# The feed-forward of a decoder layer by 2x2 blocks: seven products in place of eight

## The chip, the core and the metric

The kernel runs on one core of one Trainium2 chip. The metric is the device time of one launch in microseconds. Before the change it is 1752.19 us, the median of three runs (1750.87 to 1752.77).

## What is computed

One pre-norm decoder layer on 1024 tokens of width 1024, in float32: four causal token mixers with gates and an output projection, then a SwiGLU feed-forward of hidden width 2816, then a final RMSNorm. The change concerns the second sub-layer and its neighbours.

```python
D_MODEL = 1024; SEQ = 1024; FFN_HIDDEN = 2816; RMS_EPS = 1e-6

def rmsnorm(x, g):
    y = x * lax.rsqrt(jnp.mean(x * x, axis=-1, keepdims=True) + RMS_EPS)
    return y * g

def hybrid_layer(x, ...):
    h = rmsnorm(x, norm1_g)
    ...
    x = x + merged @ w_o
    h2 = rmsnorm(x, norm2_g)
    g_ff, up_ff = jnp.split(h2 @ w_gate_up, 2, axis=-1)
    return x + (jax.nn.silu(g_ff) * up_ff) @ w_down

def reference(x, ...):
    return rmsnorm(hybrid_layer(x, ...), final_g)
```

## The kernel before

Matrix products are made of float32r operands. `split` (L126) cuts a float32 tile into a high part (a cast on ScalarE) and a low part (a subtraction on VectorE), and `mm3` (L119) adds high by high, high by low and low by high in one PSUM bank, so a float32 product of 128 x 128 by 128 x 512 costs three matmuls (L122 to L124). Weights are laid out on the host in blocks of 128 rows by 1024 float32, loaded on SyncE's queue and split by `load_w` (L111).

The program runs through norm1, the mixers, and then twice, once for each half of 512 tokens, through the gates, the merge and the output projection `wo` (`tok_out`, L645). `evict_o` (L730) adds its PSUM banks to x; the sum, x2, lies in a tile of pool `gp` and is stored to DRAM as `x2d` on SyncE's queue. For the first half of tokens, norm2 (`norm_T`, L164) runs beside the second half's gates. The second half's x2 is loaded back from `x2d` in the feed-forward and its norm2 runs there (L745), each of its four tiles of 128 tokens with eight transposes on TensorE in two PSUM banks.

The feed-forward (L750 to L810) runs once for each half of tokens. A hidden block of 128 channels needs two weight blocks, gate and up, of 8 x 3 matmuls each (`group`, L174); Silu on ScalarE, a product on VectorE and a split give `fft`, which stays in SBUF. Then `tok_out` multiplies by `wd`, 11 weight blocks for each 512 output columns, four PSUM banks at once. The feed-forward has 2112 matmuls in gate and up and 1056 in down, 3168 in all, and 32 transposes. The last evictions, the final norm and the stores of `out` are the tail (L782 to L808).

Engines run their instructions in the order in which the program writes them, after a list scheduler has merged what the loops issue; within one engine nothing passes an instruction that waits. Tiles of a pool tag rotate through a fixed number of buffers, and a pool that is closed gives its memory to the next one, whose tiles wait for whatever last used that memory.

## Time and profile before

| | |
|---|---|
| median of three runs | 1752.19 us |
| profiled execution | 1752.49 us |
| its span, first to last instruction | 1750.5 us |
| mean granted TensorE clock | 0.998 |
| feed-forward, first matmul to last | 1006.57 to 1743.5 us |
| PE busy, share of the span | 1714.4 us, 98% |

The profiled execution has its own time, 1752.49 us: 1750.5 us of span and 2.0 us around it. It lies 0.3 us above the median. PE is TensorE's matmuls, PEld its weight loads (which overlap them), DVE VectorE, ACT ScalarE, POOL GpSimd and SP SyncE. A matmul's record in the timeline is longer than the distance to the next one, since matmuls are pipelined; the rate is read from counts in windows.

### The profile page before, as it was taken

The page shows a single profiled execution, that of the slowest core. Times are in us where ns is not written, and L with a number is a line of the kernel's source. Part 1 is how long each engine was busy: PE and PEld are TensorE (multiplying, and loading weights), DVE is VectorE, ACT ScalarE, POOL GpSimd, SP SyncE. Part 2 cuts the span into 40 slices and gives each one's busy share as a digit, 9 for nine tenths or more (in the row PEclk, how much of TensorE's full clock was granted, in tenths as well). Part 3 has the DMA queues.
Part 4 walks back from the last instruction along what each step waited for, and adds up shares of the span by engine and source line. Part 5 has one row for each costly group of instructions (what it writes and reads, how often), then busy time and mean ns, then how long its engine had stood idle before and what let it go on. Part 6 is the DMA issues. An engine that isn't in the chain of part 4 may idle for free.

```text
span 1750.5 us, 19973 instructions
## 1 busy us (share of the span) xinstructions
PE 1714.4 (98%) x7973; PEld 1392.1 (80%) x7973; DVE 816.4 (47%) x1168; ACT 605.9 (35%) x975; POOL 57.3 (3%) x124
## 2 busy tenths in 40 slices
PE   7999999999999999999999999999999999999998
PEld 7778777777788888888888888888888888888886
DVE  6676778777624345343436353333323333333232
ACT  5433456655432222243222142222212322222222
POOL 2011011010000000000000000000000000000000
PEclk9999999999999999999999999999999999999999
DMA  4311110111242224442223363222222522222222
GB/s 179 106 55 49 66 32 22 31 32 33 79 132 97 95 87 143 145 132 97 96 97 134 105 242 109 96 89 93 96 96 97 192 97 96 94 90 94 97 96 97
DMA packets 52620, 171.22 MB, mean 98 GB/s; under 512 B 6160, under 2 KB 9264, under 8 KB 52528
## 3 DMA queue, kind: packets, MB, share of 16 engines
q1 hardware_dynamic: 51952, 167.85, 28.6%
q10 hardware_dynamic: 576, 2.10, 0.4%
q8 instruction: 63, 1.03, 0.2%
q14 instruction: 29, 0.24, 0.0%
HBM read 156.27 MB, written 13.65 MB: 97 GB/s over the span
## 4 chain that ended last, share of the span: by engine, by line
PE 87%; DVE 4%; issue 1%; ACT 1%; POOL 0%; POOLq 0%; DVEq 0%; ACTq 0%
PE mmf L124 9%; PE mmf L123 9%; PE mmf L122 9%; PE mmg L124 7%; PE mmg L123 7%; PE mmg L122 7%; PE acc L124 6%; PE acc L122 6%; PE acc L123 6%; PE mm L124 3%; PE mm L122 3%; PE mm L123 3%; PE o L399 2%; PE pr L123 2%; PE pr L122 2%; PE pr L124 2%
## 5 line engine op out<-in xcount | busy, mean ns | idle before, releaser
L128 DVE TENSOR_TENSOR wlo<-wraw,whi 128x1024 fp32r<-128x1024 f32 x250 | 306.1, 1224 | 601.9 <-ACT whi L127 595.3
L127 ACT CAST whi<-wraw 128x1024 fp32r<-128x1024 f32 x250 | 262.1, 1048 | 863.2 <-PE mmf L123 320.0
L124 PE MATMUL mmf<-g0h,wlo 128*128 128x512 f32 x352 | 139.2, 396 | 0.0
L124 PE MATMUL mmf<-g1h,wlo 128*128 128x512 f32 x352 | 139.2, 395 | 0.0
L123 PE MATMUL mmf<-g1l,whi 128*128 128x512 f32 x352 | 138.7, 394 | 0.0
L123 PE MATMUL mmf<-g0l,whi 128*128 128x512 f32 x352 | 138.7, 394 | 0.0
L122 PE MATMUL mmf<-g0h,whi 128*128 128x512 f32 x352 | 138.5, 393 | 0.0
L124 PE MATMUL acc<-whi,fft 128*128 128x512 f32 x352 | 138.4, 393 | 0.0
L122 PE MATMUL acc<-whi,fft 128*128 128x512 f32 x352 | 138.3, 393 | 0.0
L122 PE MATMUL mmf<-g1h,whi 128*128 128x512 f32 x352 | 138.2, 393 | 0.0
L123 PE MATMUL acc<-wlo,fft 128*128 128x512 f32 x352 | 137.4, 390 | 0.0
L124 PE MATMUL mmg<-h1h,wlo 128*128 128x512 f32 x256 | 101.4, 396 | 0.1
L124 PE MATMUL mmg<-h0h,wlo 128*128 128x512 f32 x256 | 101.3, 396 | 0.0
L123 PE MATMUL mmg<-h0l,whi 128*128 128x512 f32 x256 | 100.9, 394 | 0.0
L123 PE MATMUL mmg<-h1l,whi 128*128 128x512 f32 x256 | 100.8, 394 | 0.0
L122 PE MATMUL mmg<-h1h,whi 128*128 128x512 f32 x256 | 100.8, 394 | 0.0
L122 PE MATMUL mmg<-h0h,whi 128*128 128x512 f32 x256 | 100.4, 392 | 0.0
L761 DVE TENSOR_TENSOR sl<-mmf,sl 128x512 f32<-128x512 f32 x44 | 30.4, 691 | 150.1 <-PE mmf L124 150.1
L122 PEld LDWEIGHTS mmf<-g1h,whi 128*128 128x128 f32 x352 | 66.6, 189 | 15.3
L122 PEld LDWEIGHTS mmf<-g0h,whi 128*128 128x128 f32 x352 | 66.6, 189 | 15.1
L123 PEld LDWEIGHTS mmf<-g1l,whi 128*128 128x128 f32 x352 | 66.1, 188 | 15.5
L123 PEld LDWEIGHTS mmf<-g0l,whi 128*128 128x128 f32 x352 | 66.1, 188 | 15.3
(253 smaller groups left out, 3187.8 us busy)
## 6 DMA issues: line engine op xcount, KB each, us to landing
wraw<-in_wgu_dram SPq DMA_DIRECT2D x88, 512.0 KB, 3.2
wraw<-in_wgate_dram SPq DMA_DIRECT2D x64, 512.0 KB, 3.2
wraw<-in_wd_dram SPq DMA_DIRECT2D x44, 512.0 KB, 3.2
wraw<-in_wmix_dram SPq DMA_DIRECT2D x22, 512.0 KB, 3.3
wraw<-in_wbr_dram SPq DMA_DIRECT2D x16, 512.0 KB, 3.2
wraw<-in_wo_dram SPq DMA_DIRECT2D x16, 512.0 KB, 3.2
xt<-in_x_dram SPq DMA_DIRECT2D x8, 512.0 KB, 9.2
yr<-ydr SPq DMA_DIRECT2D x8, 512.0 KB, 4.3
```

Of the source, the lines that this page charges most:

```text
L122: nc.tensor.matmul(o, ah, bh, start=start, stop=False)
L123: nc.tensor.matmul(o, ah, bl, start=False, stop=False)
L124: nc.tensor.matmul(o, al, bh, start=False, stop=stop)
L127: nc.scalar.copy(hi, v)
L128: nc.vector.tensor_sub(lo, v, hi.bitcast(F32))
L399: nc.tensor.matmul(o, vv[:, s0 + s, j, :], pt[:, i, s * 256:(s + 1) * 256], start=s0 + s + i == 0, stop=s0 + s + i == ns)
L761: nc.vector.tensor_mul(sl, ou, sl)
```

## The change

The feed-forward's three large products are each taken as 2x2 blocks and computed with seven block products and sums of blocks (Winograd's form), instead of eight. For gate and up, the activations are the four blocks of (token half, upper or lower 512 of the width), and each step g of 22 takes 256 of the weights' columns: seven products of 12 matmuls. For down, the blocks are (token half, even or odd hidden block) against (even or odd hidden block, 512 output columns): seven products of 11 x 12 matmuls. In all 154 x 12 + 7 x 132 = 2772 matmuls, 396 fewer.

```diff
-                nc.sync.dma_start(x2d[4 * half + t], x2[t])
+                (nc.gpsimd if half else nc.sync).dma_start(x2d[4 * half + t], x2[t])
...
+    EARLY = 10
+    def tile4(name):
+        return fp.tile([P, 1024], F32, tag="x4", name=name, bufs=10)
+    def tile2(name):
+        return fp.tile([P, HT], F32, tag="x2", name=name, bufs=6)
+    def four(s, x11, x12, x21, x22, first):
+        if first:
+            tt(s[0], x21, x22, op=add)
+            tt(s[1], s[0], x11, op=sub)
+            tt(s[2], x11, x21, op=sub)
+            tt(s[3], x12, s[1], op=sub)
...
     def norm2(t):
...
+        nc.gpsimd.dma_start(xa, xnd[t - 4])
+        nc.gpsimd.dma_start(r, x2d[t])
...
+        four(s, a0, b0, a1, b1, False)
+        yield
+        for v, to in zip([b1] + s, (h22, t1, t2, t3, t4)):
+            tr = pq.tile([P, 512], F32, tag="tr", name="trn", bufs=2).rearrange("p (k t) -> p k t", k=4)
+            for k in range(4):
+                nc.tensor.transpose(tr[:, k, :], v[:, k * P:(k + 1) * P], identf)
+            split(to[0][:, :, c], to[1][:, :, c], tr)
+    def pair_w(n=1024):
+        return [fp.tile([P, n], F32R, tag=f"w{v}{n}", name=f"w{v}", bufs=4 if n == 1024 else 1) for v in "hl"]
+    def prod(w, h):
+        o = pq.tile([P, HT], F32, tag="pp", name="pp", bufs=6)
...
+    def early(g, w):
+        nc.scalar.copy(p1, prod(half_of(w, 0), h11))
+        tt(sl, prod(half_of(w, 1), h21), p1, op=add)
+        nc.scalar.activation(sl, sl, AF.Silu)
+        nc.gpsimd.dma_start(stash[g][:, :512], p1)
+        nc.gpsimd.dma_start(stash[g][:, 512:], sl)
...
+    def rest(g, w):
...
+        tt(u2, prod(w[6], t2), p1, op=add)
+        tt(u3, prod(w[7], t3), u2, op=add)
+        p5 = prod(w[5], t1)
+        tt(u2, p5, u2, op=add)
+        tt(up, p5, u3, op=add)
+        tt(u3, prod(w[4], t4), u3, op=add)
+        tt(u2, prod(w[3], h22), u2, op=add)
+        nc.scalar.activation(u2, u2, AF.Silu)
+        nc.vector.tensor_mul(ff[:, 0], u3, sl)
+        nc.vector.tensor_mul(ff[:, 1], up, u2)
+    def down_a(j, e, o):
+        four(halves(s[0]) + halves(s[1]), e[:, 0], o[:, 0], e[:, 1], o[:, 1], True)
+        q.dma_start(ffd[j][:, 0], e[:, 0])
...
+    def down_b(j):
...
+        four(halves(s[0]) + halves(s[1]), r[0][:, :512], r[1][:, :512], r[0][:, 512:], r[1][:, 512:], False)
+            nc.gpsimd.dma_start(wdd[j][:, 3 + 2 * i:5 + 2 * i], s[i].rearrange("p (t c) -> p t c", t=2))
...
+    ready = [prepared(0), prepared(2)]
...
+        for g in range(EARLY):
+            early(g, ready.pop(0))
+            if g + 2 < EARLY:
+                ready.append(prepared(2 * g + 4))
+            if g % 2 == 0 and 1 <= g // 2 < 4:
+                next(turns[g // 2])
+            if g % 2 == 0 and g:
+                next(turns[g // 2 - 1], None)
+    nxt = blocks_w(0)
+    for g in range(NF):
+        w = nxt
+        if g + 1 < NF:
+            nxt = blocks_w(g + 1)
+        ff = rest(g, w)
+        if g % 2 == 0:
+            down_b(g // 2)
+            last = ff
+        else:
+            down_a(g // 2, last, ff)
...
+    def fetch(na, nb, j):
+        v = []
+        for src in (ffd[j][:, na], wd_of(nb, j)):
+            v.append(dn.tile([P, HT], F32, tag="dr", name="dr", bufs=8))
+            nc.sync.dma_start(v[-1], src)
+        return v
+    def operand(r):
+        hl = dn.tile([P, 2, HT], F32R, tag="dhl", name="dhl", bufs=10)
+        split(hl[:, 0], hl[:, 1], r)
+        return hl[:, 0], hl[:, 1]
+    def product(na, nb, stagger=0, raw=None):
+        acc = [pd.tile([P, HT], F32, tag="acc", name="acc", bufs=8) for _ in range(4)]
...
```

The stages of the new feed-forward are these. **Early**: products 1 and 2, which need only the first half of tokens, for the steps 0 to 9, 20 products in all; their results go to DRAM (`stash`) on GpSimd's queue. After the steps 2, 4, 6 and 8 of these stands one turn of norm2: four tiles of 128 tokens, each with five groups of four transposes in two PSUM banks (`tr`), 80 transposes in all. **Rest, steps 0 to 9**: five products each. **Rest, steps 10 to 21**: seven products each. In every step VectorE also makes four block sums of the weights (`four` in `blocks_w`) and, by turns, four of the down weights (`down_b`) or of the activations (`down_a`); these go to DRAM (`wdd`, `ffd`) on GpSimd's queue, in four or in seven pieces of 256 KB. **Down**: seven products of 11 steps j; each j loads two tiles of 256 KB from DRAM on SyncE's queue and splits both; eight PSUM banks hold two products; block results are added by VectorE, some by GpSimd.

Memory: the pools of the weights and of the feed-forward's tiles are closed and opened so that new tiles lie over old ones. In the built program the first weights' high part (`wh_8019`) begins at byte 137,216 of each partition, and the tile that holds x2's last two token tiles (`x2_7708`) ends at byte 137,600. The cast that writes `wh_8019` therefore waits for two stores on GpSimd's queue, those of `x2d` 6 and 7.

**ScalarE where the feed-forward begins.** The names `whi` and `wh` are high parts of weights, `raw` their float32, `pp` and `mmf` PSUM banks of products. Before:

```order
L127 CAST whi_7898<-wraw_7896 128x1024
L127 CAST whi_7928<-wraw_7926 128x1024
L127 CAST whi_7970<-wraw_7968 128x1024
L127 CAST whi_8001<-wraw_7999 128x1024
L127 CAST whi_8062<-wraw_8060 128x1024
```
After the change:

```order
L134 CAST whi_7906<-wraw_7904 128x1024
L134 CAST whi_7936<-wraw_7934 128x1024
L913 DMA wh_8031<-in_norm2_g_dram 128x512
L913 DMA wl_8032<-in_norm2_g_dram 128x512
L134 CAST wh_8019<-raw_8021 128x1024
L134 CAST wh_8025<-raw_8027 128x1024
L159 ACTIVATE xn2_8039,ss_8040<-x2r_8037 128x1024
L839 COPY p1_8052<-pp_8054 128x512
```
The last cast of `wo` (`whi_7928` before, `whi_7936` now) was followed by casts of gate and up weights into buffers of their own. Now the loads of norm2's weights and the cast of `wh_8019`, the one that waits for the two stores, follow it, and all that ScalarE does for the feed-forward stands behind.

**VectorE in the first norm2 turn.** `trn` are the transposes' PSUM banks, `g1l` and `t2l` to `t4l` the low parts that they end in, `tok` the sums of token blocks. Before:

```order
L128 TENSOR_TENSOR wlo_8094<-wraw_8091,whi_8093 128x1024
L147 TENSOR_SCALAR ss_8130<-ss_8130 128x1
L128 TENSOR_TENSOR g1l_7703<-trn_8046,g1h_7702 128x4x128
L128 TENSOR_TENSOR g1l_7703<-trn_8053,g1h_7702 128x4x128
L166 SCALAR_TENSOR_TENSOR xn2_8129<-x2r_8127,ss_8130,g_sb_8036 128x1024
```
After the change, from the scaling of the second token tile (whose part `wl_8164` of a weight stands just ahead) to the end of the first turn:

```order
L793 SCALAR_TENSOR_TENSOR xn2_8173<-x2r_8171,ss_8174,wl_8032 128x512
L778 TENSOR_TENSOR tok_8180<-xn2_8173,xa2_8169 128x512
L840 TENSOR_TENSOR sl_8131<-pp_8146,p1_8130 128x512
L779 TENSOR_TENSOR tok_8180<-xn2_8173,tok_8180 128x512
L780 TENSOR_TENSOR tok_8181<-xn2_8173 128x512
L781 TENSOR_TENSOR tok_8181<-xa2_8169,tok_8180 128x512
L135 TENSOR_TENSOR g1l_7711<-trn_8186,g1h_7710 128x4x128
L135 TENSOR_TENSOR g1l_7711<-trn_8193,g1h_7710 128x4x128
L135 TENSOR_TENSOR t2l_7982<-trn_8200,t2h_7981 128x4x128
L135 TENSOR_TENSOR t3l_7984<-trn_8207,t3h_7983 128x4x128
L135 TENSOR_TENSOR wl_8255<-raw_8256,wh_8254 128x1024
L135 TENSOR_TENSOR t4l_7986<-trn_8214,t4h_7985 128x4x128
```
Two low parts for a tile of 128 tokens became five (`g1l` for the block itself and for its first sum, `t2l` to `t4l` for the other sums). Ahead of the first of them stand the scalings and sums of the next tile of tokens (`tok_8180`, `tok_8181`) and the eviction of a product 2 (`sl_8131`), and a weight's low part (`wl_8255`) stands among them.

**VectorE where gate and up give way to down.** `ff` is the activation of a step, `fs` the sums for down, `dhl` the split operands of down's first steps j. Before, in the first half of tokens, the split activation `fft` was the operand itself, and the weights of down (from `wlo_9594` on) were split ahead:

```order
L761 TENSOR_TENSOR sl_9538<-mmf_9513,sl_9538 128x512
L128 TENSOR_TENSOR wlo_9594<-wraw_9591,whi_9593 128x1024
L128 TENSOR_TENSOR fft_9473<-sl_9538,fft_9473 128x512
L128 TENSOR_TENSOR wlo_9624<-wraw_9621,whi_9623 128x1024
L128 TENSOR_TENSOR wlo_9654<-wraw_9651,whi_9653 128x1024
```
After the change:

```order
L882 TENSOR_TENSOR u2_11469<-pp_11529,u2_11469 128x512
L886 TENSOR_TENSOR ff_11544<-up_11513,u2_11469 128x512
L773 TENSOR_TENSOR fs_11547<-ff_11423,ff_11544 128x512
L775 TENSOR_TENSOR fs_11548<-ff_11423 128x512
L774 TENSOR_TENSOR fs_11547<-fs_11547,ff_11423 128x512
L776 TENSOR_TENSOR fs_11548<-ff_11544,fs_11547 128x512
L135 TENSOR_TENSOR dhl_11591<-dr_11575,dhl_11591 128x512
L135 TENSOR_TENSOR dhl_11594<-dr_11577,dhl_11594 128x512
L135 TENSOR_TENSOR dhl_11613<-dr_11609,dhl_11613 128x512
```
The low parts of the first j, which down's first product needs (`dhl_11591` and `dhl_11594`), stand behind the last step's two evictions (`u2_11469` and `ff_11544`, which waits for Silu) and the four sums of `down_a`.

## Rows read from the trace of the kernel before

**Rows 1.** The profile's page: busy time, share and instructions; then the last chain.
```profile
PE 1714.4 (98%) x7973; PEld 1392.1 (80%) x7973; DVE 816.4 (47%) x1168; ACT 605.9 (35%) x975; POOL 57.3 (3%) x124
...
PE 87%; DVE 4%; issue 1%; ACT 1%; POOL 0%; POOLq 0%; DVEq 0%; ACTq 0%
```

**Rows 2.** The waits view: engine and tile, awaited, us in total, times, longest us.
```profile
ACT whi L127 <- PE mmf L123: 320.0, 82, 4.3
...
PE o L399 <- DVE pt L128: 13.0, 11, 1.9
```

**Rows 3.** Windows: start and end us, length, busy time (count) per engine, PEclk, DMA share, GB/s.
```profile
1006.57:1254.90 248.33, 247.88 (x1088) 201.63 (x1087) 91.65 (x103) 79.31 (x104) 2.19 (x4) 1.00 0.36 123
...
1621.40:1743.50 122.10, 122.07 (x530) 99.07 (x528) 35.86 (x43) 28.81 (x38) 1.31 (x3) 1.00 0.27 90
...
1400.00:1600.00 200.00, 200.00 (x865) 162.51 (x864) 67.23 (x73) 57.32 (x73) 0.00 (x0) 1.00 0.29 95
```

**Rows 4.** Timeline of PE in norm2: start us, length, line, operation, count, idle before.
```profile
1020.85 1.07 PE L161 MATMUL trn<-identf,xn 128*128 128x128 f32 x8 [0.45 <-DVE xn L166]
```

**Rows 5.** Timeline around the feed-forward's start, by engine: PE, DVE, ACT.
```profile
1006.34 0.39 PE L124 MATMUL acc<-whi,mgt 128*128 128x512 f32 x1
1006.57 0.39 PE L122 MATMUL mmf<-g0h,whi 128*128 128x512 f32 x1
...
1005.39 0.69 DVE L732 TENSOR_TENSOR x<-acc,x 128x512 f32<-128x512 f32 x1 [0.67 <-PE acc L124]
...
1006.77 0.69 DVE L732 TENSOR_TENSOR x<-acc,x 128x512 f32<-128x512 f32 x1 [0.69 <-PE acc L124]
...
1006.77 1.05 ACT L127 CAST whi<-wraw 128x1024 fp32r<-128x1024 f32 x1 [4.50 <-PE acc L124]
```

**Rows 6.** DMA issues: destination, source, queue, count, KB each, median us to landing.
```profile
wraw<-in_wgu_dram SPq DMA_DIRECT2D x88, 512.0 KB, 3.2
...
x2d<-x SPq DMA_DIRECT2D x8, 512.0 KB, 5.2
...
out_dram<-xr SPq DMA_DIRECT2D x16, 256.0 KB, 2.2
...
zc<-zdr SPq DMA_DIRECT2D x4, 256.0 KB, 3.1
```

**Rows 7.** Groups by form from 440 us on, DVE then ACT: busy us, mean ns, idle before.
```profile
L128 DVE TENSOR_TENSOR wlo<-wraw,whi 128x1024 fp32r<-128x1024 f32 x228 | 279.2, 1225 | 590.7 <-ACT whi L127 585.2 <-PE trn L161 1.8
L761 DVE TENSOR_TENSOR sl<-mmf,sl 128x512 f32<-128x512 f32 x44 | 30.4, 691 | 150.1 <-PE mmf L124 150.1
...
L166 DVE SCALAR_TENSOR_TENSOR xn<-x2r,ss,g_sb 128x1024 f32<-128x1024 f32 x4 | 5.1, 1282 | 2.2 <-POOL ss L148 2.2
...
L127 ACT CAST whi<-wraw 128x1024 fp32r<-128x1024 f32 x228 | 239.1, 1049 | 828.6 <-PE mmf L123 320.0 <-PE acc L124 232.1 <-PE mmg L123 197.5
...
L127 ACT CAST g1h<-trn 128x512 fp32r<-128x512 f32 x8 | 4.5, 587 | 0.1
```

**Rows 8.** Timeline of DVE in a merge, each row fed by the one ahead of it.
```profile
810.11 0.69 DVE L709 TENSOR_TENSOR pr_sb<-pr_sb 128x512 f32<-128x512 f32 x1
810.79 0.69 DVE L705 TENSOR_TENSOR pr_sb<-pr,sig 128x512 f32<-128x512 f32 x1
811.51 0.69 DVE L709 TENSOR_TENSOR pr_sb<-pr_sb 128x512 f32<-128x512 f32 x1
```

**Rows 9.** Windows at the kernel's start and where the mixers end.
```profile
12.00:16.00 4.00, 3.87 (x25) 3.37 (x25) 3.86 (x6) 3.27 (x7) 1.62 (x1) 1.00 1.03 421
...
440.00:460.00 20.00, 16.49 (x85) 13.45 (x84) 18.44 (x21) 8.71 (x17) 0.21 (x1) 0.91 0.07 21
```

More of the change, by code (lines that the diff above doesn't have):

```diff
@@ L180, in tile_hybrid_trunk @@
     x2d = [dp.tile([P, D], F32, name=f"x2d{t}") for t in range(8)]
+    xnd = [dp.tile([P, D], F32, name=f"xnd{t}") for t in range(4)]
     p1 = ExitStack()
@@ L663, in tok_out @@
                         kp + k2 == 0, kp == nkp - 1 and k2 == 1)
-            with in_order() if last and ch else nullcontext():
-                for t in range(4):
-                    evict(t, ch, acc[t])
+            for t in range(4):
+                evict(t, ch, acc[t])
     p2 = ExitStack()
@@ new lines, in tile_hybrid_trunk @@
+    ready = [prepared(0), prepared(2)]
+    g2 = pair_w(512)
+    for i in range(2):
+        g2[i] = g2[i].bitcast(F32)
+        nc.scalar.dma_start(g2[i], norm2_g[i * 512:(i + 1) * 512].partition_broadcast(P))
+    turns = [norm2(4 + i) for i in range(4)]
+    next(turns[0])
+    with in_order([(nc.tensor, "matmul"), (nc.tensor, "transpose")]):
+        for g in range(EARLY):
[6 more added lines that the diff above has]
+                next(turns[g // 2 - 1], None)
@@ new lines, in tile_hybrid_trunk @@
+    nxt = blocks_w(0)
+    last = None
+    for g in range(NF):
[6 more added lines that the diff above has]
+            last = ff
+        else:
+            down_a(g // 2, last, ff)
+    p3.close()
+    p0.close()
+    pqs.close()
+    dn = ctx.enter_context(tc.tile_pool(name="dn", bufs=2, reuse_waits="tile"))
+    ssf = [sp.tile([P, 2], F32, tag="ssf", name="ssf", bufs=8) for _ in range(8)]
@@ new lines, in product @@
+    def product(na, nb, stagger=0, raw=None):
+        acc = [pd.tile([P, HT], F32, tag="acc", name="acc", bufs=8) for _ in range(4)]
+        todo = [(j, t) for j in range(NJ) for t in range(4)]
+        if stagger:
+            m = 4 * (NJ - stagger)
+            todo[m:] = sorted(todo[m:], key=lambda jt: (jt[1], jt[0]))
+        ops = {}
+        for j, t in todo:
+            if j not in ops:
+                ops[j] = [operand(r) for r in raw or fetch(na, nb, j)]
+                raw = None
+                if late and j >= 2:
+                    late.pop(0)()
+            (ah, al), b = ops[j]
+            tl = slice(t * P, (t + 1) * P)
+            mm3(acc[t], (ah[:, tl], al[:, tl]), b, j == 0, j == NJ - 1)
+        return acc
@@ new lines, in keep, with load_xr, load_gf @@
+    def keep(name):
+        return [dn.tile([P, HT], F32, tag=name, name=name, bufs=4) for _ in range(4)]
+    xr, gf = [], []
+    def load_xr(t):
+        xr.append(dn.tile([P, D], F32, tag="xr", name="xr", bufs=8))
+        nc.sync.dma_start(xr[t], x2d[t])
+    def load_gf():
+        gf.append(load_g(dn, final_g, "gf", 1))
+    late = [load_gf] + [lambda t=t: load_xr(t) for t in range(8)]
+    first = fetch(0, 0, 0)
+    u2, u3 = keep("u2"), keep("u3")
+    pool_add = lambda o, v: nc.gpsimd.tensor_tensor(o, o, v, op=add)
@@ new lines, in tile_hybrid_trunk @@
+    X = product(0, 0, raw=first)
+    p1 = keep("p1")
+    for t in range(4):
+        nc.scalar.copy(p1[t], X[t])
+        pool_add(xr[t][:, lo_], p1[t])
+    X = product(1, 1)
+    for t in range(4):
+        tt(xr[t][:, lo_], X[t], xr[t][:, lo_], op=add)
+        first_half(t, lo_)
+    X = product(4, 4)
+    for t in range(4):
+        tt(u2[t], X[t], p1[t], op=add)
+    X = product(5, 5)
+    for t in range(4):
+        tt(u3[t], X[t], u2[t], op=add)
+        pool_add(xr[4 + t][:, lo_], u3[t])
+        pool_add(xr[4 + t][:, hi_], u3[t])
@@ new lines, in tile_hybrid_trunk @@
+    X = product(3, 3)
+    for t in range(4):
+        tt(u2[t], X[t], u2[t], op=add)
+        tt(xr[4 + t][:, hi_], X[t], xr[4 + t][:, hi_], op=add)
+        pool_add(xr[t][:, hi_], u2[t])
+        first_half(4 + t, hi_)
+    X = product(2, 6)
+    for t in range(4):
+        tt(xr[4 + t][:, lo_], X[t], xr[4 + t][:, lo_], op=add)
+        square(4 + t, lo_, 1)
+        rstd_f(4 + t)
+        store_f(4 + t, hi_)
+    X = product(6, 2, stagger=3)
+    with in_order():
+        for t in range(4):
+            tt(xr[t][:, hi_], X[t], xr[t][:, hi_], op=add)
+            square(t, hi_, 1)
+            for fn, i in {0: (), 1: ((rstd_f, 0), (store_f, 0), (rstd_f, 1), (store_f, 1)), 2: ((rstd_f, 2),),
+                          3: ((store_f, 2), (rstd_f, 3), (store_f, 3))}[t]:
+                fn(*((i,) if fn is rstd_f else (i, lo_)))
```

201 lines of the change are left out of this document (130 added, 71 removed).

## The prediction

> **What bounds the kernel now.** Begin with the busy shares and the last chain [rows 1]: TensorE works in 1714.4 of 1750.5 us, and 87% of the chain that ended last is TensorE's own work. Then look at who waits for whom [rows 2]: ScalarE waits 320.0 us for matmuls, while the longest sum of TensorE's own waits is 13.0 us, in the mixers. In the feed-forward TensorE is busy 247.88 of 248.33 us in the first gate and up and 122.07 of 122.10 us in the last down; VectorE is busy 91.65 us in the former, and DMA has a share of 0.36 [rows 3]. So there a matmul saved is time saved, as long as the other engines keep up. The clock stood at its full level, 2.4 GHz, in all three windows.
>
> **Price of a matmul.** 865 matmuls in 200.00 us [rows 3] give 0.2312 us each. The feed-forward's 3168 matmuls make 732 us at that rate, near the 737 us of the stage. 2772 stay: 396 x 0.2312 = 91.6 us less. Norm2's transposes rise from 32 to 80; eight take 1.07 us [rows 4], so 48 more cost 6.4 us. TensorE alone gives -85.2 us. The rest is what TensorE will now wait for.
>
> **A, the stage's start: +7.5 us.** Before, the feed-forward's first matmul follows the last of `wo` without a gap, 1006.57 after 1006.34 [rows 5], as its weights had been split long before. Now the first cast waits for the stores of x2's last two tiles. Their last addition runs at 1006.77 and takes 0.69 us, ending at 1007.46 [rows 5]. A store of this kind has a median of 5.2 us to its landing [rows 6], the cast takes 1.05 us and the low part, which the third matmul needs, 1.22 us [rows 7]. That makes 1007.46 + 5.2 + 1.05 = 1013.7 for the first matmul instead of 1006.57, 7.1 us, and 0.8 us more before the third (1.22 less two matmuls). That is 7.9 in all. The median is of stores issued four at a time, which lengthens it; the two that count here are further apart. I take 7.5, though GpSimd's queue has no row here, with 5.5 (a landing as quick as a load's 3.2 us) and 12 as ends. The Trainium skill, "DMA: Bandwidth & Descriptors", in the table at its head gives a first byte after about 1 us from GpSimd against 0.6 us from SyncE; by it A would be 0.4 us longer. No run here shows it yet.
>
> **B, four turns of norm2: +11 us.** With two banks the third group of transposes waits until the first is evicted: 0.53 for its four transposes, 0.59 for the cast and 0.69 for the subtraction [rows 4, 7], 1.8 us, where two groups' transposes took 1.07. Carried through five groups this leaves 1.45 us idle per turn, 5.8 for four: the lower end. But VectorE has, right ahead of the first eviction, a product's eviction that only then becomes ready, and three sums of the next tile, 4 x 0.67, or 2.7 us, so that the first subtraction ends some 1.6 us late. That gives about 3 us per turn; with a little less in a turn whose sums are done early, 11 in all. The upper end, 20, adds to each turn a wait for the reload, the square and the scaling (1.28 [rows 7]) of the next tile.
>
> **Rest, steps 0 to 9: +3 us.** TensorE needs 60 x 0.2312 = 13.87 us a step. VectorE has 20 operations in each: 19 of 512 columns and one of 1024. Operations that feed each other start 0.68 to 0.72 us apart [rows 8]; one of 512 is recorded at 0.691 and one of 1024 at 1.225 us [rows 7]. With 0.65 to 0.69 each, 12.4 to 13.1, plus 1.2, this is 13.6 to 14.3 us: as much as TensorE. In the ten steps 0 to 4 us from that alone; a wait of VectorE for Silu, about 0.9 us a step, which nothing fills, makes the upper end 13. I take 3.
>
> **Rest, steps 10 to 21: 0.** TensorE needs 84 x 0.2312 = 19.4 us a step, VectorE two operations more, 15.5 to 16.2 us. Loads and stores in two of the first ten steps are eight tiles of 512 KB (four of weights, two of the stash, two of down) and eleven pieces of 256 KB, 7.1 MB in 27.7 us, 255 GB/s; the most that a window shows is 421 GB/s at a full share [rows 9]. If the stores on GpSimd's queue held up buffers, it would be here; see the rivals.
>
> **C, from gate and up to down: +6 us.** After the last product VectorE has the eviction (0.69), a wait for Silu (about 0.8), a product (0.69), four sums, and then the two low parts without which TensorE's second matmul can't start: 8 x 0.67 + 0.8 = 6.2 us, less one matmul. Before, the operands were ready. The ends are 5 and 8.
>
> **Down: 0, and 10 as the upper end.** A step j is 12 matmuls, 2.77 us, for 2 x 256 KB, 189 GB/s, and four j are in flight. A load of 256 KB took 3.1 us and a store of that size 2.2 [rows 6], well within 11 us of lead. VectorE's two low parts take 1.4 of 2.77 us. In the first product the eight tiles of x2 come on top, 378 GB/s for some steps, near the 421 above, hence the upper end. The tail stays as it is.
>
> **Clock: +2 us.** In a window of 20 us in which TensorE idled for 3.5 us the clock read 0.91 [rows 9]: 3.6 us at the lower level, 1.2 GHz, a loss of at most 1.8. After A and after C I take 1 us each; the ends are 0 and 6.
>
> **Sum.** -85.2 + 7.5 + 11 + 3 + 6 + 2 = -55.7 us. The profiled execution has 1752.5 us, which makes 1696.8; the median of the runs is 0.3 lower, so I predict **1696 us**. All lower ends together give -85.2 + 5.5 + 5.8 + 0 + 5 + 0 = -68.9, or 1683; all upper ends -85.2 + 12 + 20 + 13 + 8 + 10 + 6 = -16, or 1736.
>
> **Rivals.**
> *Everything stays hidden.* The wait in A is not met, since the store lands before the low part would be ready anyway, and VectorE does its sums ahead of the turns: -85.2 + 5.8 + 5 = -74, some 1678 us. Against it: the order in which ScalarE and VectorE stand.
> *VectorE becomes the bound.* If each step of the first ten loses the wait for Silu and more, 3 us, and the turns and the first product of down go at their upper ends: -85.2 + 9 + 20 + 30 + 8 + 6 + 3 = -9, up to 1743; half of the excess gives 1720. For it: 13.6 to 14.3 us beside 13.87. Against it: the single operation's spacing in a row of independent ones is shorter than its record.
> *The loads of down go one after the other*: slower than before. If two loads of 256 KB didn't overlap, a step j would take 2 x 2.2 us or more in place of 2.77: 77 x 1.6 = 125 us, so 1696 + 125 = 1821. It decides once a pair needs over 2.77 us of the queue, and it makes the kernel slower from 2.77 + 55.7/77 = 3.5 us on. Against it: the window with 421 GB/s, in which loads of 512 KB plainly overlap. The Trainium skill, "DMA: Bandwidth & Descriptors", section "Bandwidth", wants transfers of 1 MiB for three quarters of the peak; these are of a quarter of that size, and no run here shows small ones in a dense row.
> *GpSimd's queue is slow*: slower too. In two steps it issues seven stores; buffers turn over behind them. If the queue took 4.7 us apiece, 33 us in place of 27.7 in the first steps and as much more in the later ones, eleven pairs would lose 5.3 us each, 58 us, and nothing would be gained: about 1755. No row of a GpSimd DMA stands in this trace; SyncE's stores of 512 KB landed in 5.2 us with four under way, so that one queue needn't wait for a landing.
> *The change doesn't do what it says*: the order of TensorE's instructions has the smaller number of matmuls, so only the placing of memory can fail, and for one tile it does (A).
>
> **Chances.** My forecast, within 1680 to 1710, 0.68; all hidden, below 1680, 0.09; VectorE as the bound, 1710 to 1745, 0.16; loads in a row 0.04; GpSimd's queue 0.03. The range goes from 1676 to 1724 and leaves out about 0.2: half of the third case, the last two, and a little of the second. A measurement can tell 0.2%, 3.5 us, from no change. Faster: the first three, 0.93, less 0.01 for the far end of the third; no change 0.02; slower 0.06.
>
> **What would show it.** Right: fewer matmuls by 396 at 0.231 us; a gap of 7 to 8 us at the start, with ScalarE's cast waiting for a store; about 3 us at each turn, ended by VectorE's low parts; steps of 13.9 to 14.3, then of 19.4 us; a gap of 6 us ahead of down. Wrong: gaps within the later steps or within down's products, ended by DMA; a clock that stays at its lower level for more than a few us; steps of 16 us in the first ten.

## The result, and the profile after

The changed kernel takes **1703.22 us** (median of four runs, 1701.78 to 1712.56) against 1751.58 us for the kernel before beside it (1750.87 to 1752.77): a ratio of 0.9734, 95% interval 0.9699 to 0.977. Forecast were 1696 us and a range of 1676 to 1724. The profiled execution after has 1703.8 us with a span of 1701.8 us, 48.7 us less than before; the sums below are made against it.

The page of the changed kernel, to be held against [rows 1]: busy time, last chain, and two rows of stores on GpSimd's queue (count, KB each, median us to landing) beside loads of the same size on SyncE's.

```profile
PE 1629.0 (96%) x7625; PEld 1324.7 (78%) x7625; DVE 1063.3 (62%) x1630; ACT 637.8 (37%) x1101; POOL 144.3 (8%) x253
...
PE 77%; DVE 10%; ACT 3%; issue 2%; DMA 2%; POOL 0%; POOLq 0%; DVEq 0%; ACTq 0%; SPq 0%
...
raw<-in_wgu_dram SPq DMA_DIRECT2D x54, 512.0 KB, 4.2
...
wdd<-fs POOLq DMA_DIRECT2D x22, 512.0 KB, 3.5
ffd<-fs POOLq DMA_DIRECT2D x22, 512.0 KB, 6.2
```

TensorE still holds most of the chain, 77% after 87%; VectorE is busy in 62% of the span after 47%. What TensorE now waits for stands in the waits view of the changed kernel (engine and tile, awaited, us in total, times, longest us):

```profile
PE pp L145 <- ACT wh L134: 9.6, 1, 9.6
PE trn L145 <- DVE g1l L135: 8.3, 4, 2.4
PE trn L145 <- DVE t2l L135: 3.2, 4, 1.1
PE acc L130 <- DVE dhl L135: 3.1, 1, 3.1
PE acc L129 <- ACT dhl L134: 2.5, 1, 2.5
...
PE pp L129 <- DVE u L875: 1.0, 1, 1.0
```

These are the places that the prediction named: the start of the stage (A), the four turns of norm2 (B, two rows), and the change to down (C, two rows). Within the later steps one wait of 1.0 us is left.

**A.** The timeline of the changed kernel around the start, by engine (PE, ACT), and of its critical chain the piece that decides; compare [rows 5]:

```profile
1012.65 0.40 PE L131 MATMUL acc<-whi,mgt 128*128 128x512 f32 x1
1022.67 0.79 PE L145 MATMUL pp<-g0h,wh 128*128 128x512 f32 x1 [9.62 <-ACT wh L134]
...
1021.57 1.99 ACT L134 CAST wh<-raw 128x1024 fp32r<-128x1024 f32 x2 [18.56 <-DMA x2d<-x]
...
1014.06 7.33 DMA x2d<-x
```

ScalarE's cast waits for the last store of x2 as forecast; that store took 7.33 us to its landing, where the prediction took the 5.2 us of [rows 6].

**B.** The first turn in TensorE's timeline of the changed kernel, and VectorE's operations ahead of the first eviction:

```profile
1044.93 1.25 PE L145 MATMUL trn<-identf,tok 128*128 128x128 f32 x8 [2.39 <-DVE g1l L135]
...
1041.78 0.69 DVE L840 TENSOR_TENSOR sl<-pp,p 128x512 f32<-128x512 f32 x1 [0.17 <-PE pp L145]
1042.39 0.68 DVE L779 TENSOR_TENSOR tok<-xn,tok 128x512 f32<-128x512 f32 x1
1042.98 0.69 DVE L780 TENSOR_TENSOR tok<-xn 128x512 f32<-128x512 f32 x1
1043.59 0.69 DVE L781 TENSOR_TENSOR tok<-xa,tok 128x512 f32<-128x512 f32 x1
1044.19 1.28 DVE L135 TENSOR_TENSOR g1l<-trn,g1h 128x512 fp32r<-128x512 f32 x2
```

A product's eviction and three sums stand ahead of the eviction that TensorE waits for, as counted. The four turns' gaps come to 12.0 us.

**C.** TensorE's first matmuls of down in the changed kernel:

```profile
1472.21 0.49 PE L129 MATMUL acc<-dhl 128*128 128x512 f32 x1 [2.53 <-ACT dhl L134]
1475.76 0.80 PE L130 MATMUL acc<-dhl 128*128 128x512 f32 x1 [3.06 <-DVE dhl L135]
1476.35 0.63 PE L131 MATMUL acc<-dhl 128*128 128x512 f32 x1
1476.78 0.63 PE L129 MATMUL acc<-dhl 128*128 128x512 f32 x1
```

The last two starts are 0.43 us apart, not 0.23: that is the clock. Windows of the changed kernel (columns as in [rows 3]) give its level, 0.50 being 1.2 of 2.4 GHz; the last two are the undisturbed middle of gate and up and of down:

```profile
1015.00:1020.00 5.00, 0.00 (x0) 0.00 (x0) 0.00 (x0) 0.00 (x0) 0.67 (x2) 0.71 0.96 357
1020.00:1025.00 5.00, 2.29 (x5) 1.38 (x6) 2.35 (x2) 3.04 (x4) 0.00 (x0) 0.50 0.59 238
1475.00:1480.00 5.00, 4.24 (x10) 3.41 (x11) 4.32 (x8) 0.62 (x1) 0.34 (x1) 0.50 0.96 330
...
1280.00:1380.00 100.00, 100.00 (x443) 82.79 (x442) 80.33 (x118) 28.98 (x42) 11.31 (x21) 1.00 0.46 162
...
1520.00:1620.00 100.00, 100.00 (x443) 82.80 (x442) 64.62 (x95) 44.80 (x82) 12.74 (x8) 1.00 0.64 203
```

The same windows of the kernel before, which there lie in the second half's gates, in down (all but the last few us) and in gate and up:

```profile
820.00:920.00 100.00, 100.00 (x433) 81.19 (x432) 37.75 (x43) 28.19 (x36) 0.00 (x0) 1.00 0.29 95
1280.00:1380.00 100.00, 100.00 (x436) 81.42 (x434) 30.36 (x39) 24.89 (x36) 1.65 (x3) 1.00 0.31 101
1520.00:1620.00 100.00, 100.00 (x434) 81.24 (x432) 33.70 (x36) 28.75 (x36) 0.00 (x0) 1.00 0.28 94
```

Here is what the prediction had not foreseen at all. In gate and up and in down 443 matmuls touch a window of 100 us, where 434 and 436 did before. By the distance of neighbours a matmul takes 0.2267 us, where it took 0.2317 in gate and up and 0.2303 in down, 0.2312 in the mean [rows 3]. TensorE was fully busy in both. Nothing in the diff speaks of a faster matmul.

**The balance**, profiled execution against profiled execution:

| | forecast us | measured us |
|---|---|---|
| last matmul of `wo`, 1006.34 to 1012.65 | 0 (no term) | +6.3 |
| matmuls: 3168 x 0.2312 to 2772 x 0.2267 | -91.6 | -104.0 |
| transposes, 48 more | +6.4 | +6.4 (not measured apart) |
| A, gap | +7.5 | +9.8 |
| B, four turns' gaps | +11 | +12.0 |
| steps 0 to 21, gaps | +3 | +1.1 |
| C, two gaps | +6 | +6.0 |
| down, gaps | 0 | 0 |
| matmuls at the lower clock | +2 | +3.6 |
| last matmul to the program's end, 7.4 to 14.0 | 0 (no term) | +6.6 |
| left over | | +3.5 |
| sum | -55.7 | -48.7 |

The left-over is by difference: transposes at the lower clock, first matmuls behind a gap and gaps under 0.3 us are in it, and I did not take it apart. Three lines stand out, and the experiments went to them first: the faster matmul, the 6.6 us at the end, the 6.3 us ahead of the stage.

### The profile page after: what moved, and what is told of

It is laid out like the page before. It is cut to its first block, busy times and chain, and to the rows that moved or that the text cites. A ratio compares the mean times of both kernels' runs of the same rounds, so it can differ in the third digit from the quotient of the medians.

```text
span 1701.8 us, 20554 instructions
## 1 busy us (share of the span) xinstructions
PE 1629.0 (96%) x7625; PEld 1324.7 (78%) x7625; DVE 1063.3 (62%) x1630; ACT 637.8 (37%) x1101; POOL 144.3 (8%) x253
## 4 chain that ended last, share of the span: by engine, by line
PE 77%; DVE 10%; ACT 3%; issue 2%; DMA 2%; POOL 0%; POOLq 0%; DVEq 0%; ACTq 0%; SPq 0%
PE mmg L130 6%; PE mmg L129 6%; PE mmg L131 6%; PE acc L130 6%; PE acc L131 6%; PE acc L129 6%; PE pp L129 5%; PE pp L130 5%; PE pp L131 5%; PE pp L145 3%; PE mm L131 3%; PE mm L129 3%; PE mm L130 3%; PE o L408 2%; PE pr L131 2%
## 5 line engine op out<-in xcount | busy, mean ns | idle before, releaser
L135 DVE TENSOR_TENSOR wlo<-wraw,whi 128x1024 fp32r<-128x1024 f32 x118 | 144.3, 1223 | 271.2 <-ACT whi L134 268.4
L134 ACT CAST whi<-wraw 128x1024 fp32r<-128x1024 f32 x118 | 123.6, 1048 | 349.9 <-PE mmg L130 199.7
L135 DVE TENSOR_TENSOR dhl<-dr,dhl 128x512 fp32r<-128x512 f32 x154 | 108.4, 751 | 69.2 <-ACT dhl L134 69.2
L134 ACT CAST dhl<-dr 128x512 fp32r<-128x512 f32 x154 | 89.0, 620 | 95.3 <-PE acc L131 63.4
L130 PE MATMUL acc<-dhl 128*128 128x512 f32 x308 | 121.2, 394 | 3.1 <-DVE dhl L135 3.1
L129 PE MATMUL acc<-dhl 128*128 128x512 f32 x308 | 120.9, 393 | 2.5 <-ACT dhl L134 2.5
L131 PE MATMUL acc<-dhl 128*128 128x512 f32 x308 | 120.8, 392 | 0.0
L129 PE MATMUL mm<-h0h,whi 128*128 128x512 f32 x176 | 74.7, 424 | 0.0
L129 PE MATMUL mm<-h1h,whi 128*128 128x512 f32 x176 | 73.1, 416 | 0.0
L131 PE MATMUL mm<-h0h,wlo 128*128 128x512 f32 x176 | 70.9, 403 | 0.5 <-DVE wlo L135 0.5
L130 PE MATMUL mm<-h0l,whi 128*128 128x512 f32 x176 | 71.3, 405 | 0.0
L130 PEld LDWEIGHTS acc<-dhl 128*128 128x128 f32 x308 | 58.5, 190 | 16.1 <-DVE dhl L135 3.8
L129 PEld LDWEIGHTS acc<-dhl 128*128 128x128 f32 x308 | 58.4, 190 | 15.0 <-ACT dhl L134 3.0
```

Of the source, the lines that this page charges most:

```text
L129: nc.tensor.matmul(o, ah, bh, start=start, stop=False)
L130: nc.tensor.matmul(o, ah, bl, start=False, stop=False)
L131: nc.tensor.matmul(o, al, bh, start=False, stop=stop)
L134: nc.scalar.copy(hi, v)
L135: nc.vector.tensor_sub(lo, v, hi.bitcast(F32))
```

## The experiments

### Is it the addresses? The kernel before with aligned operands

My theory was that a matmul's time depends on where its operands lie. In the changed feed-forward every tile of operands begins at a multiple of 2048 bytes of its partition, and the operands in it at multiples of 512. Before, the weights' parts begin 128 to 320 bytes past a multiple of 512. The first test leaves the kernel before as it is and moves its tiles alone.

```diff
-        hi = wp.tile([P, PW], F32R, name="whi")
-        lo = wp.tile([P, PW], F32R, name="wlo")
+        hl = wp.tile([P, 2176], F32R, name="whl")
+        hi, lo = hl[:, :n], hl[:, n:2 * n]
```

The pool `hp` is also opened ahead of `wp`, so that all begin at multiples of 512 bytes.

> The kernel before, with nothing changed but where tiles lie: a weight's high and low part share a tile of 8704 bytes and the pool of the activations is opened first, so that every operand of the large products begins at a multiple of 512 bytes within its partition; before, weights lay at offsets of 128 to 320 and activations at 384 or 256 bytes past such a multiple. In the changed kernel a matmul of the feed-forward takes 0.2267 us, against 0.2317 before in gate and up, 0.2303 in down, and the same position in a weight block has the same step in each of 17 repetitions. Theory: the addresses make the difference; then the step is 0.2267 in gates and feed-forward here too, and with some 5800 matmuls of 512 columns at 0.004 to 0.005 us less the time falls by 25 to 30 us, to 1722 to 1727. Rival: the step belongs to the new loops (products of 12 matmuls, six banks in turn); then it stays at 0.2317 and the time at 1751.6.

Measured: 1725.7 us (1725.28 to 1726.69), ratio 0.9845 (0.983 to 0.986). The same instructions are 27 us faster than in the kernel before beside it (1752.75 us). In the windows of this kernel, in gates, mostly in down and mostly in gate and up, the count is 443 everywhere; in the kernel before the same three have 433, 436 and 434, as shown above:

```profile
820.00:920.00 100.00, 100.00 (x443) 82.81 (x442) 42.81 (x51) 29.69 (x38) 0.00 (x0) 1.00 0.29 96
1280.00:1380.00 100.00, 100.00 (x443) 82.84 (x442) 34.79 (x45) 28.83 (x42) 2.20 (x4) 1.00 0.41 141
1520.00:1620.00 100.00, 100.00 (x443) 82.80 (x442) 32.73 (x35) 27.47 (x34) 0.00 (x0) 1.00 0.30 98
```

### The counter-test, and A: first weights off the memory of x2

Two kernels took A apart, and one of them also undid the alignment. In both no weight lies over a tile of x2 that is still being stored. The first takes the first product's tile ahead of the weights:

```diff
+    first = tile2("p1")
     ready = [prepared(0), prepared(2)]
```

> The changed kernel, with the small tiles p1, sl, u and up laid ahead of the weights' buffers, so that it is the first p1 and not the first weights that lies over x2's last bytes; addresses stay multiples of 2048. Theory: the gap at the start is the wait of the first weights' cast for x2's last store. Then the 9.8 us of idle TensorE go, and with them some 2.6 us of its lower clock behind the gap, less 1 to 3 us that the second or third weights may now be late, whose loads start only after wo: 1703.2 - 9 to -12, so 1691 to 1694. Rival: the load of the first weights or of x2's reload would be late anyway, and the gap only shrinks by 2 or 3 us: about 1700.

The second leaves that order as it was and puts a pad of 384 bytes ahead of the weights instead. It pushes them past x2's end, and it moves the weights of gate and up off the multiples of 512; the activations and all of down stay where they were:

```diff
+    fp.tile([P, 96], F32, name="pad", bufs=1)
```

> The changed kernel, with the first weights pushed clear of x2 by 384 bytes of padding instead. Its waits are those of the run with p1 first, but the weights of gate and up now begin 384 bytes past a multiple of 512; the activations and all of down stay where they were. Theory of addresses: 1848 matmuls of gate and up at 0.230 to 0.233 in place of 0.2267, 6 to 11 us more than the run with p1 first, about 1700; the step in down stays 0.2267. Rival, that the step belongs to the loops: the same time as the run with p1 first, within 2 us.

Measured: 1707.96 us (1703.17 to 1710.42) without the pad, 1716.52 us (1711.58 to 1718.15) with it, 8.6 us more. The padded kernel has 432 matmuls in the 100 us of gate and up, one every 0.2324 us, and 442 in down, which the pad does not move:

```profile
1280.00:1380.00 100.00, 100.00 (x432) 81.04 (x432) 79.30 (x116) 28.26 (x41) 10.15 (x19) 1.00 0.46 158
1520.00:1620.00 100.00, 99.99 (x442) 82.46 (x441) 67.10 (x99) 45.71 (x85) 13.97 (x9) 1.00 0.63 199
```

With the run before, that settles the addresses: they make the price, in both directions. In the padded kernel the weights alone were moved, so their address is enough to do it; which distances cost how much was not tried.

On A both kernels say that clearing the first weights is worth nothing here; the 9 to 12 us that were expected did not come. The gap at the start falls from 9.8 to 1.6 us, and ten microseconds later another of 9 us stands. ScalarE and TensorE in the kernel without the pad:

```profile
1023.00 1.06 ACT L159 ACTIVATE xn<-x2r 128x1024 f32<-128x1024 f32 x1 [21.36 <-DMA x2r<-x2d]
...
1031.29 0.80 PE L145 MATMUL pp<-g0h,wh 128*128 128x512 f32 x1 [8.86 <-ACT wh L134]
```

The square of norm2's first tile stands ahead of the next weight's cast on ScalarE, and it waits for x2's way out to memory and back. The placing of the weights was not the only wait there; behind it stood the reload. In the padded kernel the two gaps are 1.6 and 7.3 us.

### Can the reload be given more time?

In the next kernel, with the first weights clear as in the first of these two, norm2's four tiles start after the steps 1, 3, 5 and 7, and their turns stand after the steps 3, 5, 7 and 9:

```diff
-    next(turns[0])
...
-            if g % 2 == 0 and 1 <= g // 2 < 4:
+            if g % 2 == 1 and g // 2 < 4:
                 next(turns[g // 2])
```

> The changed kernel with p1 laid ahead of the weights, as in the run before it, and norm2's turns a step later: the first tile's square, scaling and sums follow step 1 of the early products in place of standing ahead of step 0, and the turns of transposes follow steps 3, 5, 7 and 9. With p1 ahead alone, the gap at the start shrank from 9.8 to 1.6 us, and a gap of 9.0 us opened at the third step, where the cast of weights stood on ScalarE behind the square that waits for x2's reload (landing at 1022.9, 10.9 us after its issue). Theory: that order on ScalarE and VectorE is all that is left of the cost; then the second gap goes too, TensorE's lower clock with it, and the kernel gains 9 to 12 us over the changed one, 1691 to 1694. Rival: the loads of the next weights are late as well, since stores, reloads and loads share the DMA engines there (357 GB/s); then a gap of 3 to 6 us stays at the third or fourth step and the time is 1697 to 1700.

Measured: 1708.69 us (1707.85 to 1709.94), no gain where 9 to 12 us were expected. The gaps went into the turns. TensorE's waits in this kernel:

```profile
PE trn L145 <- DVE g1l L135: 14.7, 4, 7.8
...
PE trn L145 <- DVE t2l L135: 7.8, 3, 5.0
```

VectorE's evictions of one turn stand behind the next tile's sums, and those behind its reload. The wait moved, and what stands behind it on its engine waited with it.

### B: a third bank for the transposes

```diff
-            tr = pq.tile([P, 512], F32, tag="tr", name="trn", bufs=2)
+            tr = pq.tile([P, 512], F32, tag="tr", name="trn", bufs=3)
...
-        o = pq.tile([P, HT], F32, tag="pp", name="pp", bufs=6)
+        o = pq.tile([P, HT], F32, tag="pp", name="pp", bufs=5)
```

> The changed kernel with three PSUM banks for transposes and five for products, in place of two and six. The gaps of the four turns are 2.4 and 0.9, 1.8 and 1.1, 2.4 and 0.7, 1.9 and 0.9 us, 12.0 in all. Theory: the first gap of a turn is VectorE's late first eviction, behind a product's eviction and sums, and a third bank puts it off by one group of transposes, 0.5 us, while the second, which two banks set, goes: about 6 us of the 12 stay. Rival: two banks set both; then nearly all 12 us go. In either case five banks for products suffice, as a product's eviction has 4 x 2.7 us.

Measured in a single execution: 1712.78 us. The turns' gaps fall from 12.0 to 6.6 us, so half of B was the two banks. But the bank was taken from the products, and there the waits view of this kernel shows a new row:

```profile
PE pp L129 <- DVE u L875: 10.3, 5, 2.5
```

In the changed kernel the same row reads 1.0 us. With five banks, five waits of about 2 us and more come through in ten steps, and six hide them. That is not because VectorE needs as long as TensorE there. In the changed kernel this is the window of the steps 0 to 9:

```profile
1106.00:1241.00 135.00, 135.00 (x596) 111.44 (x595) 118.13 (x179) 31.15 (x47) 16.71 (x32) 1.00 0.63 226
```

596 matmuls are just under ten steps of 13.6 us, and VectorE is busy for 118.13 of the 135 us, 11.9 a step; the prediction counted 13.6 to 14.3. With five banks it is the order that shows: the first eviction of a step (L875) stands on VectorE behind sums and low parts, and TensorE waits for the bank that it frees.

### The stage ahead: norm2's second half in a buffer of its own

In the changed kernel `xn2` shares its one buffer with `yr`, and the store of `xn` to memory on GpSimd's queue holds it. So ScalarE's casts of `ys` and with them those of the gates' weights come late. ScalarE and TensorE in the changed kernel:

```profile
759.83 1.06 ACT L159 ACTIVATE xn<-x 128x1024 f32<-128x1024 f32 x1 [1.42 <-DMA xnd<-xn]
...
770.99 1.05 ACT L134 CAST ys<-yr 128x1024 fp32r<-128x1024 f32 x1 [5.43 <-DMA yr<-ydr]
...
788.62 0.51 PE L131 MATMUL mmg<-h1h,wlo 128*128 128x512 f32 x1 [0.53 <-DVE wlo L135]
```

Between TensorE's starts there are seven gaps of 0.25 to 0.7 us from 755 to 796 us; the five from 781 us on make 3.3 us with the slower starts right behind them.

```diff
-gp.tile([P, D], F32, tag="yr", name="xn2", bufs=1)
+gp.tile([P, D], F32, tag="xk", name="xn2", bufs=1)
```

> The changed kernel, with the norm2 tile of the first half of tokens (which is now stored to DRAM for later use) in a buffer of its own; it shared one buffer with the tiles of y that the merge loads. Theory: in the second half's gates the store holds that buffer 3.5 us longer, the four loads of y start some 5 us later, ScalarE waits for each of them with the casts of weights behind it, and TensorE has gaps of 0.4 to 0.7 us between 781 and 796 us, 3.3 us in all, which the kernel before had not. With its own buffer these gaps go, and those at 755 and 763 us (0.9) as well: 3.5 to 4.5 us less, 1699. Rival: the gaps come from GpSimd's stores themselves, sharing the DMA engines with the loads of weights; then they stay and the time is 1703.

Measured: 1704.55 us (1699.58 to 1706.42). The gaps from 781 to 796 us are gone, so some 3 of the 6.3 us are this buffer; the two at 755 and 762 us stay (1.2 us), against the theory. In its profile the last matmul of `wo` starts at 1008.9, 3.7 us sooner, but 0.9 of that is there already at 469 us, ahead of all that the edit touches. In the timed runs it is within the spread, so a gain is not shown there. Most of the rest is again the price of a matmul. This is the window of the gates in the changed kernel, with 431 matmuls where the kernel before has 433:

```profile
820.00:920.00 100.00, 100.00 (x431) 80.71 (x430) 38.12 (x44) 28.19 (x36) 0.00 (x0) 1.00 0.30 95
```

By the distance of neighbours a matmul of the gates takes 0.2331 us after the change and 0.2316 before, 2.3 us for 1536 of them. The change opens its pools in another order, so tiles lie elsewhere there too.

### The end: is it GpSimd's queue?

From the issue of SyncE's last store, at 1747.05 us, to the end of the span the kernel before needs 3.5 us. In the changed kernel that issue is this row, 8.9 us from the end of its span of 1701.8 us:

```profile
1692.86 0.38 SPq L959 DMA_DIRECT2D out_dram<-xr  x1
```

Two runs ask whether GpSimd's DMAs make the end longer: one such DMA in the kernel before, and none in the changed kernel.

```diff
-    nc.sync.dma_start(chan_sb, chan)
+    nc.gpsimd.dma_start(chan_sb, chan)
```

> The kernel before, with one small load (14 KB of channel constants) moved from SyncE's to GpSimd's queue. After the change the span goes on for 8.5 us after the last store is issued, where it went on for 3.1 us before. Theory: using GpSimd's queue at all costs a fixed time at the program's end, so this kernel ends some 5.3 us later, about 1757, and its rows differ only behind the last store. Rival 1: the time at the end grows with the number of GpSimd's transfers (some 190 after the change), so one of them costs under 0.2 us and the time stays at 1751.6. Rival 2: the end waits for the last block additions on GpSimd or for a store; then nothing changes here either.

Measured: 1751.59 us beside 1752.75, ratio 0.9994 (0.9984 to 1.0003), span 1750.5. One transfer costs nothing. Then all of them on SyncE's queue in the changed kernel:

```diff
-        nc.gpsimd.dma_start(stash[g][:, :512], p1)
+        nc.sync.dma_start(stash[g][:, :512], p1)
...
-        q = nc.gpsimd
+        q = nc.sync
```

> The changed kernel with all of GpSimd's transfers (stores of norm2's tiles, x2 and its reloads, the stash, the sums for down) on SyncE's queue. Theory of the end: GpSimd's use as a DMA queue costs 5.3 us behind the last store, in proportion to its transfers, as one small transfer cost nothing; without them the span ends 3.1 us after the last store's issue, 8.5 us before. Rival: the end is set by something else in the new down stage, and stays at 8.5 us. For the rest of the kernel: SyncE's queue takes its entries in order, so loads of weights now stand behind stores that wait for sums. The loads have some 10 us of lead in the steps from 10 on and 4 us in the ten first; theory: gaps in the ten first steps of 0 to 2 us each, none later, in all 0 to 20 us, so 1698 to 1718. Rival: the stores land sooner from SyncE's queue and nothing is lost: 1697.

Measured: **1758.32 us** (1756.86 to 1762.66), ratio 1.004 (1.0028 to 1.0053), slower than before the change. Its last store is issued at 1752.03 in a span of 1755.2: 3.2 us, so the 5.7 us at the end are the price of GpSimd's queue when over a hundred transfers have gone over it. But without that queue the whole gain is lost. SyncE's queue in this kernel (who it waits for), and two of TensorE's rows in the waits view:

```profile
SPq L894 <- DVE ff L885: 136.0, 11, 14.2
...
PE pp L129 <- ACT wh L134: 27.3, 7, 5.4
...
PE acc L129 <- ACT dhl L134: 11.3, 1, 11.3
```

A store that waits for its data holds the loads behind it on the same queue: there is a gap of 3 to 6 us at the beginning of every step from 3 to 10, one of 11 us ahead of down, and 85 matmuls start 0.43 us ahead of the next, at the lower clock, where 17 did. The expectation had the right mechanism and a far too small price. The Trainium skill, "DMA: Bandwidth & Descriptors", in the table at its head has GpSimd's path slower to the first byte; in the profile's rows above, 512 KB stored from it land in 3.5 and 6.2 us and 512 KB loaded from SyncE in 4.2 us, so these rows show no plain order, and what decided here was which waits share a queue.

### C: the last four sums on GpSimd

```diff
+        four(halves(s[0]) + halves(s[1]), e[:, 0], o[:, 0], e[:, 1], o[:, 1], True,
+             nc.gpsimd.tensor_tensor if j == NF // 2 - 1 else tt)
```

> The changed kernel with the four sums of the last gate-and-up piece moved from VectorE to GpSimd, nothing else. Theory (term C: in the second gap of the change of stage VectorE's four sums stand ahead of the low part, 4 x 0.67 us): the gap of 3.33 us at the second matmul of the first down product goes to under 1 us, the gap of 2.7 us before it stays; the profiled span falls from 1701.8 to about 1698 (3 us of gap and 1 us of clock). Rival (the low part waits for something else, Silu or the cast on ScalarE): the 3.33 us stay within 0.5 and the span stays at 1701 to 1703. GpSimd's sums take 1.6 us each in the changed kernel; if down's first sums wait for them, a new gap of 2 to 5 us stands in the first 20 us of down.

Measured in a single execution: 1704.22 us, span 1702.3. The second gap falls from 3.33 to 1.75 us, not to under 1. The sums are gone from VectorE, but its low parts now take longer. First VectorE's and GpSimd's rows in this kernel, then VectorE's in the changed kernel:

```profile
1474.69 5.73 DVE L135 TENSOR_TENSOR dhl<-dr,dhl 128x512 fp32r<-128x512 f32 x4
1474.92 1.59 POOL L773 TENSOR_TENSOR fs<-ff 128x512 f32<-128x512 f32 x1 [2.68 <-DVE ff L886]
...
1474.42 4.90 DVE L135 TENSOR_TENSOR dhl<-dr,dhl 128x512 fp32r<-128x512 f32 x8
```

The three low parts behind the first take 1.76 us each in place of 0.69, while GpSimd's sums run, and the first of these three is one that TensorE waits for. So about 1.1 us of what the move gave was taken back. The 1.6 us that are left do not arrive at the end: from the start of the stage to C this run needs 2.3 us more than the changed kernel, with gaps of the same length. A window at the first turn in this kernel, then the same one in the changed kernel:

```profile
1040.00:1050.00 10.00, 7.11 (x35) 5.68 (x34) 7.69 (x13) 4.77 (x8) 2.75 (x5) 0.83 0.72 243
```

```profile
1040.00:1050.00 10.00, 6.81 (x40) 5.39 (x39) 8.81 (x14) 5.20 (x9) 2.05 (x4) 1.00 0.68 231
```

The same idle time lowered the clock at the first turn in one run and not in the other. The spread of the timed runs fits that. The changed kernel's run of 1701.78 us had a mean granted clock of 0.991, the one of 1712.56 us 0.984: 0.7% of 1702 us is 11.9 us, and they differ by 10.8. No profile of the slower one was taken, so where its clock fell is not shown. The kernel before, with hardly a gap from 500 us to its end, ran in 1750.87 to 1752.77 us beside it.

### All together

The last two kernels put the finds together: aligned operands ahead of the stage, the buffer of its own and the last sums on GpSimd; the second also clears the first weights and puts a turn's evictions ahead of the next tile's start. Both keep GpSimd's queue. The edits are those above, and for the order:

```diff
-            if g % 2 == 0 and 1 <= g // 2 < 4:
-                next(turns[g // 2])
             if g % 2 == 0 and g:
                 next(turns[g // 2 - 1], None)
+            if g % 2 == 0 and 1 <= g // 2 < 4:
+                next(turns[g // 2])
```

> The changed kernel with three edits: the split weights ahead of the feed-forward in one tile, so that their operands stand at multiples of 512 bytes; norm2's second half in a buffer of its own; the last sums of gate and up on GpSimd. Theory (addresses set the matmul's time, and not only in the feed-forward): aligning the whole of the kernel before gave -27 us, of which its feed-forward's 3168 matmuls hold 3168 x (0.231 - 0.2267) = 13.6, so 13.4 us are ahead of it; with 3.7 us from the buffer and 3 to 4 from the sums the kernel takes about 1703 - 20.5 = 1682 us (1678 to 1688), and the stretch of gates shows steps under 0.230 us. Rival (ahead of the feed-forward TensorE isn't what ends last, VectorE and ScalarE are): only 7 us, 1696.

> The kernel of e10_aligned_own_buffer with two more edits: the first product's tile is taken ahead of the weights, so that no weight lies over a tile of x2 that is still being stored, and norm2's evictions stand ahead of the next tile's start. Theory of the reload chain (whatever stands first, norm2's third and fourth tile wait some 8 us for x2's way through memory at the stage's start): the gap at the start goes from 9.6 to 1.6 us and one of 7 to 9 us stands some 20 us on; the time is within 4 us of e10_aligned_own_buffer. Rival (with the evictions first the reload is hidden behind products): 8 to 12 us less than e10_aligned_own_buffer, about 1672.

Measured: **1690.48 us** (1685.67 to 1691.39), ratio 0.9645 (0.9632 to 0.9658), and 1690.62 us (1687.06 to 1692.86), ratio 0.9648 (0.9635 to 0.9661). Both beat the changed kernel by 13 us, and neither the other, as the theory of the reload chain has it: the second has gaps of 1.6 us at the start and of 9.1 us twelve microseconds on. In the first the start of the last matmul of `wo` goes from 1012.65 to 995.45, 17.2 us, which is what the alignment and the buffer were to give; but from there to the last matmul it needs 679.0 us in place of 675.2, though its gaps are 2.4 us shorter. The clock takes that back and more: 33 matmuls instead of 17 run at its lower level, 3.2 us, the transposes take 1.9 us longer, and the matmuls on which the clock changes about 1 us. So 1682 was missed by the clock and by the last sums, which gave 1.6 us here too in place of 3 to 4, not by the addresses. A window of gates and one of down's start in this kernel:

```profile
820.00:920.00 100.00, 100.00 (x443) 82.80 (x442) 42.35 (x50) 28.46 (x37) 0.00 (x0) 1.00 0.31 100
...
1470.00:1480.00 10.00, 10.00 (x46) 8.27 (x45) 3.13 (x6) 3.30 (x6) 0.00 (x0) 1.00 1.04 415
```

The second row also answers a rival, the loads of down one after the other: loads on SyncE's queue, mostly in pieces of 256 KB, and the last stores on GpSimd's moved 415 GB/s together with TensorE busy throughout.

## Why the prediction was right, and where not

- **Price of a matmul.** The step that failed most. It took the 0.2312 us of [rows 3] as a property of the instruction; the aligned and the padded kernel show that it is a property of the address too. The term came out at -104.0 in place of -91.6. The trace of before held a sign of this: with nothing waiting, its steps in gate and up differ by the position in a weight block, from 0.228 to 0.236 us, which a mean over 200 us hides.
- **A.** Mechanism right, and the gap 2.3 us longer than 7.5, within its ends of 5.5 and 12: the store took 7.33 us, not 5.2. The DMA share of the window behind its issue was 0.96, and loads of weights were under way beside it; that they made it longer is likely, not shown. The text had the stores that count as further apart than before, but all four were issued 1.4 us apart, little more than the 1.1 of the kernel before. That GpSimd's own path adds 0.4 us to it, as the Trainium skill's "DMA: Bandwidth & Descriptors" would have it, no run here shows. The placing of one tile, which the text named, was half the story: cleared, the reload takes its place.
- **B.** 12.0 for 11, with the very operations that were counted ahead of the eviction. The third bank confirms that about half is the two banks.
- **Rest, steps 0 to 9.** 1.1 for 3. The count of VectorE's time, 13.6 to 14.3 us a step, was some 2 us too high: it was busy for 11.9 of 13.6. Its operations that do not feed each other start 0.60 us apart (the rows under B), where 0.65 to 0.69 was taken. VectorE as the bound, the third case, is not met. With five banks its order shows, with six it is covered.
- **Steps 10 to 21, and down.** 0 and 0, as forecast. Both DMA rivals fell: no gap in down, and GpSimd's queue kept up. The rival of a slow queue came true only in the mirror image, when its work went to SyncE.
- **C.** 6.0 for 6.
- **Clock.** 3.6 us in matmuls where 2 was taken. By the granted clocks of the timed runs it is also the term that varies from run to run, by up to some 10 us, which no single term in the sum allowed for.
- **Terms that were missing.** 6.3 us ahead of the stage, of which some 3 are the shared buffer and some 2 the slower matmuls of the gates: the diff's store of `xn` on a slow path was read for the stage that uses it and not for the buffer that it holds. And 6.6 us behind the last matmul, of which 5.7 are the price of GpSimd's queue at the program's end; "the tail stays as it is" was wrong.

So the median came 7 us above the forecast because 12.4 us of unforeseen gain met 12.9 us of unforeseen loss, and the other 6.5 are A, B, the clock and what was left over, less the 1.9 us that the steps did not lose. The gaps at A, B and C were found where the prediction had them and for the reasons it gave; the closeness of the sum is partly luck.

## What to carry to other kernels

Before pricing fewer matmuls, read the distance of neighbouring matmuls in each stage: where it differs between stages with TensorE fully busy, look at the operands' addresses first. Here moving tiles alone gave 27 us, more than half of what the whole change gave. When a wait is removed from an in-order queue, name what stands behind it, and when a store is moved to another queue, name the loads that it then stands in front of. When work goes from VectorE to GpSimd, look at what VectorE does beside it: here its operations took 1.76 us in place of 0.69. And an idle stretch of TensorE can cost twice, once by itself and once by the clock behind it, the latter not the same in each run.

## What the runs showed of the hardware that was not expected

- A 128x512 float32r matmul took 0.2267 us with operands at multiples of 512 bytes, 0.2324 us in gate and up after a shift of 384 bytes; the kernel before, 1752.75 us beside it, became 1725.7 us by moving tiles alone.
- A program that used GpSimd's queue throughout ended 8.9 us after its last store's issue, one that did not, or did once, 3.2 to 3.5 us after it.
- A subtraction of 128x512 on VectorE took 0.69 us alone and 1.76 us beside a sum of GpSimd's.
- The granted clock fell to 0.50 in or behind idle stretches of 6 to 10 us; at those of 2 to 3 us it fell in some runs and not in others.
